# Hybrid decoder step on one core: the program is recorded first and issued in an order made by a list scheduler

## The chip, the core and the metric

The kernel runs on one core of a Trainium2 chip. The core has five instruction queues that run beside one another: PE (TensorE, matmuls; its weight loads are listed as PEld), DVE (VectorE), ACT (ScalarE), POOL (GpSimd) and SP (SyncE, which here issues the transfers between memory and SBUF). Each queue runs its instructions in the order in which they stand in it, and an instruction that waits for another engine holds up all that stand behind it. The metric is the device time of one execution in microseconds (us); lower is better.

## The reference

One decoder layer (D = 1024) over a prompt of 2048 tokens and, with the same weights, over one new token each of 8 sequences. Everything is float32.

```python
def decoder_layer(x, ...):
    y = parallel_mixer(rms_norm(x, norm_mix), ...)
    x = x + y
    x = x + memory_attend(rms_norm(x, norm_mem_q), mem_k, mem_v, w_mq, w_mo)
    x = x + swiglu(rms_norm(x, norm_ffn), w_gate, w_up, w_down)

def parallel_mixer(h, ...):
    p = h @ w_in
    u = p[GLU_A] * sigmoid(p[GLU_B])                 # Conformer half, 512 channels
    c = silu(layer_norm(depthwise_conv31(u) + conv_b))
    qkv = silu(depthwise_conv4(p[QKV]))              # gated DeltaNet half, 4 heads of 128
    q, k, v = l2_norm(q), l2_norm(k), v              # chunks of 64 tokens, triangular solve,
    o = gated_delta_chunked(q, k, v, g, beta, s0)    # 128x128 state handed from chunk to chunk
    return concat(c, rms_norm(o) * silu(z)) @ w_out

def memory_attend(h, mem_k, mem_v, ...):             # 4 heads of 256, 256 memory tokens
    return softmax(q @ mem_k.T * scale) @ mem_v @ w_mo

def swiglu(h, ...):                                  # inner width 2816
    return (silu(h @ w_gate) * (h @ w_up)) @ w_down
```

After the layer comes a last `rms_norm`; the outputs are the two sequences, the projected memory, and the new convolution rows and DeltaNet states.

## The kernel before

**Work.** The prompt is cut into 4 blocks of 512 tokens (`TB`). Per block the stages are: input projection (`hd`), short convolutions, the DeltaNet chunks, the 31-tap convolution, output projection and attention (`rg`, `sc`), and the feed-forward part (FFN). To keep float32's precision on TensorE's faster path, each operand is split into a rounded half and a remainder ("hi" and "lo"), and a product is made of three matmuls of halves. A weight tile arrives by transfer as `raw`; ACT writes its hi half and POOL or DVE its lo half into `w`. There are 11 `raw` and 6 `w` slots.

**FFN.** For each pair of 128-column steps the partial products `fx`, `fy` and `fz` are made on PE in PSUM banks of those names. DVE and ACT read them out into `ffu` and `ffs`, and PE needs the bank of a product free before it starts a later one: so PE's first matmul into `fy` can wait for a DVE operation on `ffs` or `ffu`. From the results `ff` the down products (`dn`) are made and added to the residual `x` by DVE (`xd` for the 8 decode rows).

**What runs beside it.** The next blocks' mixer: the convolution `cacc`, 31 taps of one `scalar_tensor_tensor` each on DVE (480 in all); the inverse of the DeltaNet triangle, long chains of short DVE operations on `bit`, `biq`, `w16` and `x16`; transposes of keys and queries on PE into `pk` and `pq`, four slices of 128 columns in one PSUM bank, of which ACT reads each slice for itself and sums its squares (`chj`); `lnq` and `podt` are other transposes of the same kind. `hT`, `catS` and `op` are operands as they are split on DVE, `sqj` squares for a norm, `kv`, `dg`, `chv`, `osc` smaller steps of the attention and of DeltaNet.

**Order.** The program is written by generators ("lanes") that the class `Sched` resumes. The classes `Clock` and `Engine` keep a virtual time for each engine with a cost for each operation, and a lane is resumed when the virtual PE has come so far that its inputs would be there. So the text of the program is already a merge of the FFN with the mixer of later blocks. Each call goes straight to the framework as it is written (`nc.tensor.matmul(...)`, line 256; `transpose`, line 261; DVE, ACT and POOL through `Engine`, line 118; transfers, line 243); the framework gives the tiles their slots, adds the semaphores, and orders each engine's queue by the place in the program. Since all calls pass through these few lines, the profile is read by tile names rather than by lines.

Of the kernel before, what the change touches and what calls it, by code (L numbers as in the profile page):

```python
# [8 lines left out]
F32 = mybir.dt.float32  # L9
F32R = mybir.dt.float32r  # L10
AF = mybir.ActivationFunctionType
ALU = mybir.AluOpType
# [35 lines left out]
NW = 6  # L48
NT2 = 28
NACT = 22  # L50
# [15 lines left out]
NRAW = 11  # L66


class Clock:


    def __init__(self):
        self.at = {"pe": 0.0, "act": 0.0, "dve": 0.0, "pool": 0.0, "sp": 0.0, "dma": 0.0}
        self.ready, self.used = {}, {}
        self.table = None
        self.ring, self.nbank = {}, {"mm": 3, "s": 3, "o": 1, "cv": 1}
        self.held = set()
# [20 lines left out]
SETS = {AF.Sigmoid: "sigmoid", AF.Silu: "silu", AF.Exp: "exp"}  # L98


def elems(ap):
    n = 1
    for x in ap.shape[1:]:
        n *= x
    return n


class Engine:
# [5 lines left out]
    def __getattr__(self, op):  # L114
        f = getattr(self.real, op)

        def call(**kw):
            r = f(**kw)  # L118
            ins = [v for k, v in kw.items() if k not in ("out", "accum_out") and hasattr(v, "name") and hasattr(v, "shape")]
            out = kw["out"]  # L120
            src = kw.get("in_", kw.get("in0"))
            n = max(elems(out), elems(src)) if src is not None else elems(out)
            if self.name == "act":
                ns = 80 + 0.86 * n + 93 * (len(ins) - 1) + (60 if kw.get("accum_out") is not None else 0)
                t = SETS.get(kw.get("func"))
                if t and t != self.clock.table:
                    self.clock.table = t
                    ns += 1290
            elif self.name == "dve":
                fast = op in ("tensor_copy", "tensor_scalar") and src.space != bass.MemoryType.PSUM  # L130
                ptr = any(hasattr(kw.get(k), "shape") for k in ("scalar", "scalar1"))
                ns = (125 if ptr else 65) + n * (6.2 if op == "reciprocal" else 0.53 if fast else 1.05)
            else:
                ns = 300 + n * 165 if kw.get("op") == ALU.pow else 120 + n * (2.2 if op == "tensor_tensor" else 3.4)
            self.clock.run(self.name, ns, ins, out)
            if kw.get("accum_out") is not None:
                self.clock.ready[kw["accum_out"].name] = self.clock.ready[out.name]
            return r

        return call  # L140


class Sched:


# [13 lines left out]
    def add(self, gen, slack=-20.0, first=False):  # L159

        lane = [gen, self.vt, gen.__name__, slack]
        self.lanes.insert(0 if first else len(self.lanes), lane)
        return lane
# [71 lines left out]
def hybrid_step(ctx: ExitStack, tc: tile.TileContext, i: dict, o: list):  # L235
    nc = tc.nc
    C = Clock()
    V, A, G = Engine(nc.vector, "dve", C), Engine(nc.scalar, "act", C), Engine(nc.gpsimd, "pool", C)
    GS = nc.gpsimd
    S = Sched(C)  # L240

    def dma(out, in_, after=0.0):
        nc.sync.dma_start(out=out, in_=in_)
        n = 4
        for x in out.shape:
            n *= x
        C.at["sp"] = max(C.at["sp"] + 60, C.when([in_]), after)
        C.at["dma"] = max(C.at["dma"], C.at["sp"] + 1100) + max(n / 360.0, 60.0)
        C.ready[out.name] = max(C.ready.get(out.name, 0.0), C.at["dma"] + 1650)
        C.used[in_.name] = max(C.used.get(in_.name, 0.0), C.at["dma"])  # L250

    def mm(out, lhsT, rhs, start, stop, skip=False):
        n = elems(rhs)
        four = lhsT.dtype == F32 or n < 256
        S.wait(max(C.when([lhsT, rhs]), C.ready.get("free " + out.name, 0.0) if start else 0.0))
        nc.tensor.matmul(out, lhsT, rhs, start=start, stop=stop, skip_group_check=skip)  # L256
        C.run("pe", 3 + max(n, 64) * (4 if four else 1) / 2.4, [lhsT, rhs], out, 90.0)

    def transpose(out, in_, identity):
        S.wait(max(C.when([in_]), C.ready.get("free " + out.name, 0.0)))  # L260
        nc.tensor.transpose(out, in_, identity)
        C.run("pe", 110.0, [in_], out, 90.0)

    cst = ctx.enter_context(tc.tile_pool(name="cst", bufs=1))
    sm = ctx.enter_context(tc.tile_pool(name="sm", bufs=2))
    wpool = ctx.enter_context(tc.tile_pool(name="wpool", bufs=NW))
    rpool = ctx.enter_context(tc.tile_pool(name="rpool", bufs=NRAW))
    t2pool = ctx.enter_context(tc.tile_pool(name="t2pool", bufs=NT2))
    cpool = ctx.enter_context(tc.tile_pool(name="cpool", bufs=2))
    apool = ctx.enter_context(tc.tile_pool(name="apool", bufs=NACT))  # L270
    psum = ctx.enter_context(tc.tile_pool(name="psum", bufs=1, space=bass.MemoryType.PSUM))
    dram = ctx.enter_context(tc.tile_pool(name="dram", bufs=1, space=bass.MemoryType.DRAM))
    W2 = 520

    uid = [0]
# [5 lines left out]
    live = {"t2": set(), "act": set()}  # L281
# [47 lines left out]
    def const(name, shape, dt=F32):  # L329
        return cst.tile(list(shape), dt, tag=name, name=name)  # L330
# [9 lines left out]
    def load_first(ks):  # L340
        for k in ks:
            dma(x_first[k], xT[k, :, cols_of(0)])
# [5 lines left out]
    vcol_t = const("vcol", [P, rows])  # L348
    load_first((0,))
    dma(vcol_t, i["vec"])  # L350
    ones = const("ones", [P, P])
    GS.memset(ones, 1.0)
    ident = const("ident", [P, P])
    make_identity(nc, ident)
    ex = const("ex", [P, 13])
    GS.memset(ex[:, 0:4], 0.5)
    GS.memset(ex[:, 4:8], -1.0)
    GS.memset(ex[:, 8:13], -0.5)
    nhalf = ex[:, 8:12]
# [44 lines left out]
    for pair in PAIRS:  # L404
        for st in STEPS:
            k = int(st[1])
            if st[0] == "h":
                at = [O_QKV // P + g + k for g in (H, 0, 2 * H)]
# [274 lines left out]
    def three(pts, wh, wl, x, spans, first, last, skip=False):  # L683
        for w_, part in ((wh, 0), (wh, 1), (wl, 0)):
            for pt, (lo, hi) in zip(pts, spans):
                mm(pt, w_, x[:, part, lo:hi], first and w_ is wh and part == 0, last and w_ is wl, skip)
# [7 lines left out]
    def rstd(sqs, n):  # L694

        yield sqs
        yield ("ps", "s")
        nt = n // P
        pt = ps("pss", shape=(P, nt))
        for t in range(nt):  # L700
            for k, s_ in enumerate(sqs):
                mm(pt[:, t : t + 1], s_[:, t * P : (t + 1) * P], ones[:, 0:1], k == 0, k == len(sqs) - 1)
        drop(*{s_.name: s_ for s_ in sqs}.values())
        m = small("ms", [P, nt], bufs=3)
        V.tensor_scalar(out=m, in0=pt, scalar1=1e-6, scalar2=None, op0=ALU.add)
        r = small("rs1", [P, nt], bufs=3)
        G.tensor_tensor(out=r, in0=m, in1=ex[:, 8 : 8 + nt], op=ALU.pow)
        yield r
        return r

    def spread(r, n, both=False, spare=RES):

        nt = n // P
        yield ("t2", 2 + spare)
        dg = t2("dg", (P, nt, P))
        rb_ = t2("rsb")[:, :n]
        V.tensor_tensor(out=dg, in0=bc(ident, 1, [P, nt, P]), in1=bc(r, 2, [P, nt, P]), op=ALU.mult)
        yield dg
        yield ("ps", "s")
        pb = ps("prs", shape=(P, n))  # L720
        mm(pb, ones, dg.rearrange("p t j -> p (t j)"), True, True)
        drop(dg)
        A.activation(out=rb_, in_=pb, func=AF.Copy)
        if both:
            return pb, rb_
        yield rb_
        return rb_
# [175 lines left out]
    def dec_mixer():  # L903
# [110 lines left out]
        for h in range(H):  # L1014
            transpose(pvt[:, h * P : (h + 1) * P], vhl[:, h, :].bitcast(F32), ident)
# [45 lines left out]
    def scalars(b, hT, res):  # L1061
# [12 lines left out]
        for t in range(NT):  # L1074
            transpose(pb_[:, t, :], bdf[:, t * P : (t + 1) * P], ident[:16, :16])
# [31 lines left out]
        yield ("ps", "s")  # L1107
        pr = ps("pgr", shape=(NT * H, P))
        transpose(pr, gcol.rearrange("p t h -> p (t h)"), ident)
        gr = t2("gr", (NT * H, P))  # L1110
        V.tensor_copy(out=gr, in_=pr)
# [114 lines left out]
    def base_inverse(x, w, tmp_):  # L1226

        GS.memset(w, 0.0)
        GS.memset(w[:, 0:256:17], 1.0)
        V.tensor_scalar(out=w[:, 1:256:34], in0=x[:, 1:256:34], scalar1=-1.0, scalar2=None, op0=ALU.mult)  # L1230
# [315 lines left out]
    for s in LEV:  # L1546
        m = const(f"nms{s}", [P, 64])
# [124 lines left out]
    for pair in PAIRS:  # L1672
# [3 lines left out]
        for st in STEPS:  # L1676
# [8 lines left out]
            k = int(st[1])  # L1685
# [692 lines left out]
    for b in range(NB):  # L2378
# [7 lines left out]
        rest = ffn(b, ops[b], go[b])  # L2386
        ws.pool_lo, ws.ahead = False, 4
    S.until(lambda: not S.lanes, "end")


_OUTS = [
# [76 lines left out]
```

## Time and profile before

| what | value |
| --- | --- |
| median of the runs (3) | 3152.3 us (3145.48 to 3153.3) |
| the profiled execution: its time | 3143.72 us |
| its span, first to last instruction | 3142.0 us |
| PE busy | 2981.1 us, 95% (18950 records; the program has 17905 matmuls, some leave two) |
| DVE busy | 2138.6 us, 68% |
| POOL busy | 1679.4 us, 53% |
| ACT busy | 1452.5 us, 46% |
| mean DMA rate | 149 GB/s |
| mean granted TensorE clock | 0.980 |

The span leaves 1.7 us of the execution's time outside of it. PE is the engine that is nearly always busy; the other engines deliver its operands and empty its banks. A row of the groups gives a kind of instruction, its total and mean duration, and the idle time just before it with the engine that ended it.

### The profile page before, as it was taken

The numbers are of one execution on the slowest core, as the hardware profiler recorded it, in microseconds if no ns is written. First come the engines' busy times: TensorE is split into PE (matmuls) and PEld (weight loads), VectorE is DVE, ScalarE is ACT, GpSimd is POOL, SyncE is SP. The second block draws the span as 40 slices with busy tenths as digits, with TensorE's granted clock in tenths as the row PEclk, the third lists the DMA queues.
The fourth block names the chain that finished last, engine by engine and source line by source line (L and its number), as shares of the span: only waits on it lengthen the run. The fifth ranks groups of instructions, "written<-read, shape, count | busy, mean of one in ns | idle before, by whom it ended". The sixth has DMA issues, their size and how long they took to land.

```text
span 3142.0 us, 53798 instructions
## 1 busy us (share of the span) xinstructions
PE 2981.1 (95%) x18950; PEld 2639.6 (84%) x18950; DVE 2138.6 (68%) x4335; ACT 1452.5 (46%) x2909; POOL 1679.4 (53%) x1454
## 2 busy tenths in 40 slices
PE   8999989999999989889989999999999999799998
PEld 6899967888887878778877888897799998689997
DVE  7767898978797889867778655446654445663435
ACT  6533444344663435344444545444444445444443
POOL 3423444334654557666731367883147775158786
PEclk9999999999999999999999999999999999999999
DMA  5433433443884335445557455553345443245452
GB/s 182 127 107 106 136 111 126 138 132 118 265 251 140 115 111 188 135 154 174 186 168 240 141 165 182 171 170 117 127 140 155 145 156 121 71 140 156 149 158 95
DMA packets 355182, 468.73 MB, mean 149 GB/s; under 512 B 56448, under 2 KB 154688, under 8 KB 354896
## 3 DMA queue, kind: packets, MB, share of 16 engines
q1 hardware_dynamic: 354912, 465.29, 46.7%
q8 instruction: 150, 2.46, 0.3%
q14 instruction: 120, 0.98, 0.1%
HBM read 380.18 MB, written 85.57 MB: 148 GB/s over the span
## 4 chain that ended last, share of the span: by engine, by line
PE 46%; DVE 9%; POOL 5%; issue 4%; DMA 2%; ACT 1%; SPq 0%; POOLq 0%; DVEq 0%; ACTq 0%
PE dn L256 12%; PE fy L256 10%; PE rg L256 7%; PE fz L256 6%; PE fx L256 6%; PE sc L256 3%; POOL w L118 3%; DVE w L118 1%; DVE x L118 1%; DVE op L118 1%; POOL sqj L118 1%; DVE tt L118 1%; DVE cacc L118 1%; DVE xn L118 1%; PE pu L256 1%
## 5 line engine op out<-in xcount | busy, mean ns | idle before, releaser
L118 POOL TENSOR_TENSOR w<-raw,w 128x512 fp32r<-128x512 f32 x898 | 1217.8, 1367 | 704.3 <-ACT w L118 649.7
L118 ACT ACTIVATE w<-raw 128x512 fp32r<-128x512 f32 x1176 | 735.0, 630 | 1024.4 <-PE dn L256 263.3
L256 PE MATMUL dn<-ff,w 128*128 128x512 f32 (+2 forms) x2688 | 524.1, 351 | 37.4 <-DVE xd L118 16.4
L256 PEld LDWEIGHTS dn<-ff,w 128*128 128x128 f32 x2688 | 426.8, 190 | 107.8 <-issue 23.1
L256 PE MATMUL fy<-op,w 128*128 128x256 f32 (+1 forms) x3168 | 434.9, 286 | 25.6 <-DVE ffs L118 12.2
L256 PEld LDWEIGHTS fy<-op,w 128*128 128x128 f32 x3168 | 406.2, 192 | 34.3 <-DVE ffu L118 14.3
L256 PE MATMUL hd<-hT,w 128*128 128x512 f32 (+2 forms) x1920 | 406.4, 360 | 15.3 <-ACT w L118 8.3
L118 DVE SCALAR_TENSOR_TENSOR cacc<-cu,cw,cacc 128x512 f32<-128x512 f32 x480 | 358.2, 746 | 9.2 <-ACT cacc L118 4.2
L256 PEld LDWEIGHTS hd<-hT,w 128*128 128x128 f32 x1920 | 305.1, 190 | 61.1 <-ACT w L118 8.4
L118 DVE TENSOR_TENSOR x<-dn,x 128x512 f32<-128x512 f32 (+1 forms) x448 | 252.5, 570 | 124.8 <-PE dn L256 123.4
L118 POOL TENSOR_TENSOR sqj<-sqj,sqj 128x512 f32<-128x512 f32 (+1 forms) x98 | 137.9, 1407 | 327.1 <-ACT sqj L118 322.1
L118 DVE TENSOR_TENSOR w<-raw,w 128x512 fp32r<-128x512 f32 x278 | 241.0, 874 | 101.5 <-ACT w L118 99.1
L256 PE MATMUL fz<-op,w 128*128 128x256 f32 (+1 forms) x2112 | 289.5, 285 | 3.3 <-DVE ffs L118 2.0
L256 PE MATMUL fx<-op,w 128*128 128x256 f32 (+1 forms) x2112 | 285.0, 283 | 4.4 <-ACT ffu L118 1.6
L256 PEld LDWEIGHTS fx<-op,w 128*128 128x128 f32 x2112 | 268.3, 189 | 13.0 <-ACT ffu L118 2.2
L256 PEld LDWEIGHTS fz<-op,w 128*128 128x128 f32 x2112 | 268.7, 190 | 6.3 <-DVE ffs L118 2.2
L256 PE MATMUL rg<-catS,w 128*128 128x512 f32 (+1 forms) x960 | 193.5, 357 | 4.3 <-DVE x L118 3.0
L256 PE MATMUL sc<-w,hT 128*128 128x512 f32 x768 | 190.8, 403 | 6.2 <-DVE x L118 4.4
L256 PE MATMUL rg<-pT,w 128*128 128x512 f32 x768 | 190.7, 403 | 3.5 <-ACT pr L118 3.1
L118 DVE TENSOR_TENSOR ffu<-fy,ffu 128x256 f32<-128x256 f32 (+1 forms) x176 | 74.3, 422 | 169.4 <-PE fy L256 169.0
L256 PEld LDWEIGHTS rg<-catS,w 128*128 128x128 f32 x960 | 155.4, 191 | 29.8 <-DVE x L118 2.7
L256 PEld LDWEIGHTS sc<-w,hT 128*128 128x128 f32 x768 | 143.0, 190 | 41.7 <-DVE x L118 5.0
(380 smaller groups left out, 4123.4 us busy)
## 6 DMA issues: line engine op xcount, KB each, us to landing
raw<-sums SPq DMA_DIRECT2D x264, 256.0 KB, 2.7
raw<-in_w_gate_dram SPq DMA_DIRECT2D x176, 256.0 KB, 2.7
raw<-in_w_down_dram SPq DMA_DIRECT2D x176, 256.0 KB, 2.6
raw<-in_w_up_dram SPq DMA_DIRECT2D x110, 256.0 KB, 2.6
raw<-in_w_in_dram SPq DMA_DIRECT2D x96, 256.0 KB, 2.8
sums<-raw SPq DMA_DIRECT2D x88, 256.0 KB, 2.0
raw<-in_w_out_dram SPq DMA_DIRECT2D x64, 256.0 KB, 3.8
raw<-wk SPq DMA_DIRECT2D x64, 256.0 KB, 2.7
```

The source lines that it names most:

```text
L118: r = f(**kw)
L256: nc.tensor.matmul(out, lhsT, rhs, start=start, stop=stop, skip_group_check=skip)
```

## The change

What each instruction computes is left alone. The calls that the program makes are no longer passed on, but recorded on a `Tape` with their engine, operands and a cost in ns. When the whole program has been written down, `Tape.graph` works out which operation depends on which, `Tape.order` makes a new order, and `Tape.issue` makes the calls in that order, with the framework's own ordering switched off (`manual_schedule`), so that every queue keeps the order of the calls. The framework still adds the semaphores.

- The graph: an operation depends on another where they touch overlapping boxes of rows and columns of the same tile, one of them writing; matmuls into the same PSUM tile keep their order.
- The order: an event-driven list scheduler. The engine that can start earliest takes, of the operations that are ready by its clock, the one that stands first in the program as it was written (`key`). A DVE operation that needs the port shared with POOL may be passed over for another that doesn't, while POOL holds the port. A tile may be begun only if its tag has a free slot, and no tile that stands before it in the program can be locked out.
- The clocks: costs per operation, a delay from each engine to each other one (`LAT`), 1283 ns for an ACT table load, transfers in a row at 360 bytes per ns.

```diff
+class Tape:
+    LAT = {
+        "pe": dict(pe=0, dve=196, act=197, pool=210, sp=180),
+        "dve": dict(pe=149, dve=127, act=128, pool=155, sp=120),
...
+    def cost(self, eng, op, args, kw, outs, ins):
...
+            return max(max(m, 64) * 0.835, (n if n >= 256 else 4 * n) * 0.4492) + 3, False, None
...
+        if eng == "act":
+            ptr = len(ins) - 1
+            return 0.834 * n + (50 if psum_in else 94) + 93 * ptr, False, SETS.get(kw.get("func"))
...
+            return 68 + (61 if ptr else 0) + n * (6.2 if op == "reciprocal" else 0.525 if half else 1.042), big > 1, None
...
+        return 135 + n * (2.14 if op == "tensor_tensor" else 3.4), True, None
...
+    def graph(self):
+        over = lambda x, y: x[0] <= y[1] and y[0] <= x[1] and x[2] <= y[3] and y[2] <= x[3]
...
+            for a in outs:
+                if a.name in self.tag_of:
+                    b = self.box(a)
+                    for k, x in writes.get(a.name, ()):
+                        if over(b, x):
+                            p[k] = 1
+                    for k, x in reads.get(a.name, ()):
+                        if over(b, x):
+                            p[k] = 1
+                    if eng == "pe":
+                        if a.name in last_pe:
+                            p[last_pe[a.name]] = 1
+                        last_pe[a.name] = n
...
+    def order(self, key=None):
+        preds, tiles = self.graph()
+        key = key or list(range(N))
...
+        while len(done) < N:
+            best = None
+            for e in engines:
+                if avail[e]:
+                    t = clock[e]
+                elif future[e]:
+                    t = max(clock[e], future[e][0][0])
+                else:
+                    continue
+                if best is None or t < best[0]:
+                    best = t, e
...
+            ns, port, tb = self.ops[n][7]
+            s = t
+            if port and e in ("dve", "pool"):
+                s = max(s, port_at)
+                port_at = s + ns
...
+    def issue(self, tc):
+        with tc.manual_schedule():
+            for n in self.order():
+                _, _, fn, args, kw, *_ = self.ops[n]
+                fn(*args, **kw)
...
 def hybrid_step(ctx: ExitStack, tc: tile.TileContext, i: dict, o: list):
...
-    V, A, G = Engine(nc.vector, "dve", C), Engine(nc.scalar, "act", C), Engine(nc.gpsimd, "pool", C)
+    tape = Tape()
+    GS, PE, SP = tape.port(nc.gpsimd, "pool"), tape.port(nc.tensor, "pe"), tape.port(nc.sync, "sp")
...
-        nc.tensor.matmul(out, lhsT, rhs, start=start, stop=stop, skip_group_check=skip)
+        PE.matmul(out, lhsT, rhs, start=start, stop=stop, skip_group_check=skip)
...
     S.until(lambda: not S.lanes, "end")
+    tape.issue(tc)
```

The instructions are the same ones as before, but for their waits and the ACT table loads, which follow from the order (67 before, 72 now). Of PE's 17907 instructions 14348 (80%) stand at the same place of their queue as before; of DVE's, which move most after ACT's, 758 do, and the mean move is 10 places.

**Place 1: DVE, in an FFN that runs beside a triangle's inverse and a convolution; PE's `fy` waits here at 1269 us of the profile before.** `bit`, `biq`, `w16` and `x16` belong to the inverse, `cacc` to the convolution, `w` from `raw` is a weight's lo half; `ffs` from `fy` is what PE waits for. Before:

```order
L118 TENSOR_TENSOR ffu_2601_13745<-fz_2603_13748,ffu_2601_13745 128x256
L118 TENSOR_TENSOR bit_2574_13605<-w16_2569_13565,x16_2568_13564 32x512
L118 SCALAR_TENSOR_TENSOR cacc_2618_13834<-cu_2586_13640,cw_124,cacc_2618_13834 128x512
L118 TENSOR_REDUCE biq_2597_13720<-bit_2574_13605 32x64
L118 SCALAR_TENSOR_TENSOR cacc_2618_13834<-cu_2586_13640,cw_124,cacc_2618_13834 128x512
L118 TENSOR_TENSOR bit_2574_13605<-biq_2597_13720,w16_2569_13565 32x512
L118 TENSOR_TENSOR w_2617_13831<-raw_2609_13798,w_2617_13831 128x512
L118 TENSOR_REDUCE w16_2569_13565<-bit_2574_13605 32x8x8
L118 TENSOR_TENSOR w_2619_13841<-raw_2583_13632,w_2619_13841 128x512
L118 COPY x16_2568_13564<-w16_2569_13565 32x256
L118 SCALAR_TENSOR_TENSOR cacc_2618_13834<-cu_2586_13640,cw_124,cacc_2618_13834 128x512 x4
L118 TENSOR_TENSOR ffs_2602_13746<-ffu_2601_13745,fy_2608_13775 128x256
```

Now:

```order
L426 TENSOR_TENSOR ffu_2601_2799<-fz_2603_2801,ffu_2601_2799 128x256
L426 TENSOR_TENSOR bit_2574_2772<-biq_2592_2790,w16_2569_2767 32x4x4
L426 SCALAR_TENSOR_TENSOR cacc_2618_2816<-cu_2586_2784,cw_107,cacc_2618_2816 128x512
L426 TENSOR_TENSOR bit_2574_2772<-biq_2592_2790,w16_2569_2767 32x4x4
L426 TENSOR_TENSOR ffs_2602_2800<-ffu_2601_2799,fy_2608_2806 128x256
L426 TENSOR_REDUCE w16_2569_2767<-bit_2574_2772 32x2x2 x4
L426 SCALAR_TENSOR_TENSOR cacc_2618_2816<-cu_2586_2784,cw_107,cacc_2618_2816 128x512
L426 TENSOR_TENSOR bit_2574_2772<-w16_2569_2767,x16_2568_2766 32x64
L426 SCALAR_TENSOR_TENSOR cacc_2618_2816<-cu_2586_2784,cw_107,cacc_2618_2816 128x512
L426 TENSOR_TENSOR bit_2574_2772<-w16_2569_2767,x16_2568_2766 32x64
L426 TENSOR_REDUCE biq_2595_2793<-bit_2574_2772 32x16 x2
L426 TENSOR_TENSOR ffs_2602_2800<-fz_2603_2801,ffs_2602_2800 128x256
```

The operation on `ffs` and `fy` stood behind the last steps of the inverse, two weight halves and six taps that followed the operation on `ffu`, and stands behind two short operations and one tap now; nineteen operations went from ahead of it to behind it, those before the first row shown among them, and one tap went the other way.

**Place 2: DVE, in a later FFN; PE's `dn` waits here at 2136 us.** `hT` and `catS` are operands of a later stage, `x` from `dn` is the addition to the residual, and `ffu` from `fy` is what frees the bank. Before:

```order
L118 TENSOR_TENSOR ffu_4310_23069<-fz_4314_23090,ffu_4310_23069 128x256
L118 TENSOR_TENSOR ff_4315_23098<-ffu_4290_22933,ff_4315_23098 128x512
L118 TENSOR_TENSOR hT_4334_23230<-x_3426_18165,hT_4334_23230 128x512
L118 TENSOR_TENSOR ffs_4311_23070<-ffu_4310_23069,fy_4318_23112 128x256
L118 TENSOR_TENSOR ffs_4311_23070<-fz_4314_23090,ffs_4311_23070 128x256
L118 TENSOR_TENSOR ffu_4310_23069<-fy_4318_23112,ffu_4310_23069 128x256
L118 TENSOR_TENSOR x_2204_11735<-dn_4327_23187,x_2204_11735 128x512
L118 TENSOR_TENSOR x_2210_11758<-dn_4328_23195,x_2210_11758 128x512
L118 TENSOR_TENSOR sqj_4335_23233<-sqj_4335_23233,sqj_4355_23310 128x512
L118 TENSOR_TENSOR ffu_4310_23069<-fy_4318_23112,ffu_4310_23069 128x256
```

Now:

```order
L426 TENSOR_TENSOR ffu_4310_4508<-fz_4314_4512,ffu_4310_4508 128x256
L426 TENSOR_TENSOR ff_4315_4513<-ffu_4290_4488,ff_4315_4513 128x512
L426 TENSOR_TENSOR hT_4354_4552<-x_3433_3631,hT_4354_4552 128x512
L426 TENSOR_TENSOR ffs_4311_4509<-ffu_4310_4508,fy_4318_4516 128x256
L426 TENSOR_TENSOR catS_4465_4663<-cat_4464_4662,catS_4465_4663 128x512
L426 TENSOR_TENSOR ffs_4311_4509<-fz_4314_4512,ffs_4311_4509 128x256
L426 TENSOR_TENSOR catS_4467_4665<-cat_4466_4664,catS_4467_4665 128x512
L426 TENSOR_TENSOR ffu_4310_4508<-fy_4318_4516,ffu_4310_4508 128x256
L426 TENSOR_TENSOR x_2204_2402<-dn_4327_4525,x_2204_2402 128x512
L426 TENSOR_TENSOR catS_4469_4667<-cat_4468_4666,catS_4469_4667 128x512
L426 TENSOR_TENSOR x_2210_2408<-dn_4328_4526,x_2210_2408 128x512
L426 TENSOR_TENSOR ffu_4310_4508<-fy_4318_4516,ffu_4310_4508 128x256
```

Three operations on `catS` of 512 columns now stand ahead of the second `ffu` from `fy`, and one on `sqj` went behind it.

**Place 3: PE, in an input projection (at 127.78 us of the profile before), with the waits.** Four transposes of keys (`kT`) go into slices of one bank, `pk`. Before:

```order
L256 MATMUL hd_250_1540<-hT_69_441,w_194_1192 128x264
L256 MATMUL hd_249_1539<-hT_69_441,w_194_1192 128x256
L256 MATMUL hd_250_1540<-hT_69_441,w_194_1192 128x264
L261 MATMUL pk_254_1602<-ident_94,kT_235_1470 128x128 [waits DMAHW5_49]
L261 MATMUL pk_254_1602<-ident_94,kT_235_1470 128x128 x3
L256 MATMUL hd_249_1539<-hT_71_447,w_194_1192 128x256
L256 MATMUL hd_250_1540<-hT_71_447,w_194_1192 128x264
```

Now:

```order
L426 MATMUL hd_249_446<-hT_69_266,w_194_391 128x256
L426 MATMUL hd_250_447<-hT_69_266,w_194_391 128x264
L426 MATMUL pk_254_451<-ident_91,kT_235_432 128x128 [waits DMAHW1_49]
L426 MATMUL pk_254_451<-ident_91,kT_235_432 128x128 x2
L426 MATMUL pk_254_451<-ident_91,kT_235_432 128x128 [waits Activation_49]
L426 MATMUL hd_249_446<-hT_71_268,w_194_391 128x256
L426 MATMUL hd_250_447<-hT_71_268,w_194_391 128x264
```

The last of the four now waits for ACT, which it did not: an ACT operation that reads another slice of the bank (`chj`) has been issued ahead of it. A transpose into `pk`, `pq`, `lnq`, `pkk` or `podt` has such a new wait at 21 places (8, 6, 4, 1 and 2), at none before.

More of the change, by code (lines that the diff above doesn't have):

```diff
@@ new lines, with __init__, __getattr__, call @@
+class TapePort:
+    def __init__(self, tape, real, eng):
+        self.tape, self.real, self.eng = tape, real, eng
+    def __getattr__(self, op):
+        fn = getattr(self.real, op)
+        def call(*args, **kw):
+            self.tape.add(self.eng, op, fn, args, kw)
+        return call
+class TapePool:
+    def __init__(self, tape, pool, bufs, psum):
+        self.tape, self.real, self.bufs, self.psum = tape, pool, bufs, psum
+    def tile(self, shape, dt, tag, name, bufs=None):
+        t = self.real.tile(shape, dt, tag=tag, name=name) if bufs is None else self.real.tile(shape, dt, tag=tag, name=name, bufs=bufs)
+        tp = self.tape
+        key = (id(self), tag)
+        tp.tag_of[t.name] = key
+        tp.bufs[key] = bufs or self.bufs
+        if self.psum:
+            tp.psum.add(t.name)
+        return t
@@ L237, in hybrid_step @@
     C = Clock()
-    V, A, G = Engine(nc.vector, "dve", C), Engine(nc.scalar, "act", C), Engine(nc.gpsimd, "pool", C)
-    GS = nc.gpsimd
+    tape = Tape()
+    GS, PE, SP = tape.port(nc.gpsimd, "pool"), tape.port(nc.tensor, "pe"), tape.port(nc.sync, "sp")
+    V, A, G = Engine(tape.port(nc.vector, "dve"), "dve", C), Engine(tape.port(nc.scalar, "act"), "act", C), Engine(GS, "pool", C)
     S = Sched(C)
     def dma(out, in_, after=0.0):
-        nc.sync.dma_start(out=out, in_=in_)
+        SP.dma_start(out=out, in_=in_)
         n = 4
@@ L260, in transpose @@
         S.wait(max(C.when([in_]), C.ready.get("free " + out.name, 0.0)))
-        nc.tensor.transpose(out, in_, identity)
+        PE.transpose(out, in_, identity)
         C.run("pe", 110.0, [in_], out, 90.0)
[L264 to L272, printed above, removed]
+    cst = tape.pool(ctx.enter_context(tc.tile_pool(name="cst", bufs=1)), 1)
+    sm = tape.pool(ctx.enter_context(tc.tile_pool(name="sm", bufs=2)), 2)
+    wpool = tape.pool(ctx.enter_context(tc.tile_pool(name="wpool", bufs=NW)), NW)
+    rpool = tape.pool(ctx.enter_context(tc.tile_pool(name="rpool", bufs=NRAW)), NRAW)
+    t2pool = tape.pool(ctx.enter_context(tc.tile_pool(name="t2pool", bufs=NT2)), NT2)
+    cpool = tape.pool(ctx.enter_context(tc.tile_pool(name="cpool", bufs=2)), 2)
+    apool = tape.pool(ctx.enter_context(tc.tile_pool(name="apool", bufs=NACT)), NACT)
+    psum = tape.pool(ctx.enter_context(tc.tile_pool(name="psum", bufs=1, space=bass.MemoryType.PSUM)), 1, True)
+    dram = tape.pool(ctx.enter_context(tc.tile_pool(name="dram", bufs=1, space=bass.MemoryType.DRAM)), 1)
     W2 = 520
```

210 lines of the change are left out of this document (added).

## The prediction

> **What bounds the kernel now.** I read the engine shares first, then the slices, the groups, the waits of PE and the timeline at the largest of them. The shares:
>
> ```profile
> PE 2981.1 (95%) x18950; PEld 2639.6 (84%) x18950; DVE 2138.6 (68%) x4335; ACT 1452.5 (46%) x2909; POOL 1679.4 (53%) x1454
> ```
>
> PE sets the time, and a new order cannot take work from it, since the matmuls stay the same. It can only fill PE's idle time, 3142.0 - 2981.1 = 161 us, and what the clock loses behind it. Where that lies, six windows tell (length, PE busy, its loads, DVE, ACT, POOL, then granted clock, DMA share, GB/s):
>
> ```profile
> 0.00:1000.00 1000.00, 954.97 (x5835) 824.07 (x5836) 821.87 (x1821) 472.64 (x1005) 422.19 (x498) 0.99 0.48 150
> 1000.00:1700.00 700.00, 639.14 (x3878) 555.61 (x3877) 555.97 (x968) 310.78 (x655) 391.05 (x308) 0.96 0.49 160
> 1700.00:2700.00 1000.00, 977.15 (x6394) 878.68 (x6393) 536.97 (x1096) 476.48 (x897) 580.43 (x431) 0.99 0.47 149
> 2300.00:2600.00 300.00, 300.00 (x2478) 298.66 (x2477) 132.11 (x398) 139.39 (x254) 228.81 (x171) 1.00 0.50 153
> 2700.00:2800.00 100.00, 79.02 (x531) 72.67 (x530) 74.77 (x187) 38.07 (x64) 30.18 (x23) 0.88 0.27 85
> 2800.00:3100.00 300.00, 300.00 (x2123) 281.05 (x2121) 124.71 (x215) 140.88 (x258) 235.01 (x176) 1.00 0.52 157
> ```
>
> Two FFN stretches of 300 us are PE from end to end at full clock: nothing is to be had there. Up to 1700 us, where DVE is 81% busy (1377.84 of 1700), PE idles 105.9 us; from 1700 to 2700 another 22.9, and 21.0 in the single piece from 2700 to 2800. PE's waits say for whom (total, times, longest):
>
> ```profile
> PE dn L256 <- DVE xd L118: 16.4, 2, 13.6
> PE fy L256 <- DVE ffs L118: 12.2, 2, 6.5
> PE fy L256 <- DVE ffu L118: 12.0, 13, 3.8
> PE dn L256 <- DVE ffu L118: 9.7, 3, 4.2
> PE pss L256 <- DVE sqj L118: 8.4, 6, 3.2
> PE hd L256 <- ACT w L118: 8.3, 2, 7.3
> ```
>
> Nearly all are DVE's, and short: no engine is too slow, but DVE does other work when PE needs a bank. So the change is worth what it does to the place of these few DVE operations in their queue.
>
> **Gains.** The 6.5 us row is place 1 of the change. The timeline there, DVE's rows and then PE's:
>
> ```profile
> 1262.57 1.00 DVE L118 TENSOR_TENSOR bit<-biq,w 32x512 f32<-32x512 f32 x1
> ...
> 1265.58 3.11 DVE L118 SCALAR_TENSOR_TENSOR cacc<-cu,cw,cacc 128x512 f32<-128x512 f32 x4
> 1268.60 0.41 DVE L118 TENSOR_TENSOR ffs<-ffu,fy 128x256 f32<-128x256 f32 x1
> ```
>
> ```profile
> 1259.31 1.68 PE L256 MATMUL fz<-op,w 128*128 128x256 f32 x12 [0.17 <-DVE ffu L118]
> ...
> 1269.06 2.93 PE L256 MATMUL fy<-op,w 128*128 128x256 f32 x12 [6.53 <-DVE ffs L118]
> ```
>
> DVE ran inverse steps and taps while PE stood; the operation PE waited for takes 0.41. The nineteen operations that go behind it last 8.77 us here, one tap of 0.75 comes ahead: 8.0 against a stall of 6.5, so it closes. What is late next: the inverse steps, whose result PE needs only in a later chunk, and the taps, which have slack until the convolution ends.
>
> I did the same for each of the 104 gaps of PE over 0.3 us that end on DVE, ACT or POOL, together 162.0 us, the first of them inside the first of these rows, the last in the second:
>
> ```profile
> 7.34 2.09 PE L256 MATMUL hd<-hT,w 128*128 128x512 f32 x4 [7.34 <-ACT w L118]
> ...
> 3133.88 1.19 PE L256 MATMUL prs<-dg,ones 128*128 128x256 f32 x2 [1.58 <-DVE dg L118]
> ```
>
> For each I took the operation waited for, with what stood ahead of it in its queue before and doesn't now, and the reverse, and likewise PE's own work moved ahead of the waiting matmul, in durations of this trace. At 55 gaps (80.3 us of stall) the balance is better, and it covers 72.1 us, 43 of them whole. At 8 (20.0 us) nothing moves. One of these is the longest of all, 13.6 us before `dn` at 2749.76:
>
> ```profile
> 2746.72 0.68 DVE L118 TENSOR_TENSOR op<-xn,op 128x512 fp32r<-128x512 f32 x1
> 2747.32 1.28 DVE L118 TENSOR_TENSOR op<-tt,op 128x512 fp32r<-128x512 f32 x2
> 2748.53 0.68 DVE L118 TENSOR_TENSOR w<-raw,w 128x512 fp32r<-128x512 f32 x1
> 2749.13 0.41 DVE L118 TENSOR_TENSOR x<-dn,x 128x256 f32<-128x256 f32 x1
> 2749.47 0.14 DVE L118 TENSOR_TENSOR xd<-dn,xd 128x4 f32<-128x4 f32 x1
> ```
>
> A norm's whole work stands ahead of `x` and `xd` there, in both kernels, so that stall stays. **Term 1: -72.** That is the most these places give; below it lies nothing at all, if what DVE has passed over becomes the next wait.
>
> **Losses.** At the other 41 gaps (61.7 us) more now stands ahead than before, by 132.6 us in all. Place 2 is one:
>
> ```profile
> 2129.61 2.48 PE L256 MATMUL dn<-ff,w 128*128 128x512 f32 x10
> 2136.31 4.09 PE L256 MATMUL dn<-ff,w 128*128 128x512 f32 x10 [4.21 <-DVE ffu L118]
> ```
>
> ```profile
> 2126.53 0.69 DVE L118 TENSOR_TENSOR x<-dn,x 128x512 f32<-128x512 f32 x1 [0.71 <-PE dn L256]
> 2134.18 1.73 DVE L118 TENSOR_TENSOR sqj<-sqj,sqj 128x512 f32<-128x512 f32 x1 [6.96 <-POOL sqj L118]
> 2135.84 0.41 DVE L118 TENSOR_TENSOR ffu<-fy,ffu 128x256 f32<-128x256 f32 x1
> ```
>
> `hT` and `catS` operations of 4.1 us come ahead there and `sqj` (1.73) goes behind. But DVE stood idle for 6.96 us just before, waiting for POOL with `sqj` at the head of its queue; if the work moved ahead runs in that time it costs nothing, and `ffu` even goes earlier. Bounds for the 132.6: nearly none (a twentieth, 7), or all. I take a fifth, 27, because the list fills time in which its clock sees DVE free, and its costs agree with rows of this trace where I can hold them together:
>
> ```profile
> L256 PE MATMUL dn<-ff,w 128*128 128x512 f32 (+2 forms) x2688 | 524.1, 351 | 37.4 <-DVE xd L118 16.4
> L118 DVE SCALAR_TENSOR_TENSOR cacc<-cu,cw,cacc 128x512 f32<-128x512 f32 x480 | 358.2, 746 | 9.2 <-ACT cacc L118 4.2
> L118 POOL TENSOR_TENSOR w<-raw,w 128x512 fp32r<-128x512 f32 x898 | 1217.8, 1367 | 704.3 <-ACT w L118 649.7
> ```
>
> It charges 233 ns for a 512-column matmul, and the ten at 2129.61 took 2.48 with the last one's drain in it; 662 for a tap, of 746 measured with its overlap; 1231 for POOL's half, of 1367. Errors of a tenth stay within a gap's length where the order was made with DVE free, but DVE is 81% busy before 1700 us, so not all of it can be. **Term 2: +27.**
>
> **New waits.** At 21 places PE now waits between two transposes for a reader of another slice of the same bank (place 3). Before, these readers came when they could. What one such wait costs, the keys' transposes show, first all of them, then place 3's own in the timeline and by tile:
>
> ```profile
> L261 PE MATMUL pk<-ident,kT x64: 270/272/329, 99.9 to 1347.4; 128*128 128x128 f32 x64
> L118 ACT ACTIVATE chj<-pk x64: 252/277/278, 103.2 to 1353.2; 128x128 bf16<-128x128 f32 x64
> L118 ACT ACTIVATION_READ_ACCUMULATOR chj<-pk x64: 191/195/214, 103.3 to 1353.4; 128x1 f32 x64
> ```
>
> ```profile
> 127.78 0.60 PE L261 MATMUL pk<-ident,kT 128*128 128x128 f32 x4
> ```
>
> ```profile
> L118 ACT ACTIVATE chj<-pk x4: 258/272/277, 134.9 to 138.3; 128x128 bf16<-128x128 f32 x4
> ```
>
> If ACT is there at once, PE loses the read's 0.28 us: 21 x 0.28 = 6. If ACT is as late as it was before, it loses that lateness: 3.3 us at the first group of four, 5.8 at the last, 7.1 at place 3, and 3.4 on average over the 32 groups of keys and queries: 21 x 3.4 = 71. Everything in PE's queue stands behind such a wait, the projection's matmuls above all. In the new order ACT's `chj` stands directly behind one weight half (0.63, first row below), no longer behind an activation that itself waited for DVE, so I take a read with its accumulator (0.28 + 0.20) and that half ahead of it, 1.1 to 1.2 us each: **term 3: +25**, nearer to the low end for that reason.
>
> ```profile
> L118 ACT ACTIVATE w<-raw 128x512 fp32r<-128x512 f32 x1176 | 735.0, 630 | 1024.4 <-PE dn L256 263.3 <-issue 151.1 <-PE rg L256 110.1
> L118 ACT ACT_TABLE_LOAD x67 | 86.0, 1283 | 10.6 <-DMA vcol<-in_vec_dram 4.8 <-issue 2.8 <-DVE du L118 1.8
> ```
>
> The Trainium skill speaks against the change here: its page "PSUM — Partial Sum Buffer", section "PSUM bank collisions raise a hardware error", asks that PSUM be guarded by bank and quadrant, not by address, whichever engines read or write. The change's graph goes by address, so by that rule its list counts on overlaps that it will not get. The 21 waits in the new order agree; with a price of 3.4 us each for them the sum is that of the third rival below.
>
> **Clock.** Behind 1269.06 the twelve matmuls took 2.93 us, the twelve at 1259.31 took 1.68: a stop that long costs some 1.25 us more in clock. Seven gaps of over 3 us are closed whole: 7 x 1.25 = 9. **Term 4: -9**, between 0 (new stops as long) and -25 (the 0.96 of 1000 to 1700 loses 28 us, most of it regained).
>
> The Trainium skill's page "TensorE: Matmul & The Clock Gate", Part 1, has the clock halved only after an idle window of about 3.4 us. By that rule just three of the seven stops would have cost anything; term 4 would be an estimated -4, and the sum 3119.7. The 6.53 us stop agrees with it, and none of the rows here tells the two counts apart.
>
> **The rest.** Five more table loads cost ACT 5 x 1.28 by the second row above, on an engine 46% busy. SP issues as many transfers as before, and DMA at half its share covers their new places; its queue is in order, so a load that waits for a `raw` slot holds those behind it, and if that made a weight late, ACT's `w` and PE's `hd` would be late with it, as the 7.3 us in the row of `hd` and ACT's `w` shows. Recording the program happens before the chip runs and costs it nothing.
>
> **Sum**, against the profiled execution: 3143.7 - 72 + 27 + 25 - 9 = 3114.7. The median of the runs stands 8.6 above that execution, so 3123 for the median.
>
> **Rivals.**
> *DVE has no room.* Of the work moved ahead four fifths count, as DVE is 81% busy up to 1700 us: -72 + 106 + 25 - 9 = +50, 3202. It decides from a share of 42% on ((72 + 9 - 25) / 132.6). For it: the busiest windows are those in which most of this work lies. Against it: DVE's idle time there, 322 us, is more than twice the 132.6.
> *The waits only move.* 80% of PE's instructions keep their place, ties go by the old program order, and a filled stall hands the wait to the next thing that is late; gains halve, -36 + 27 + 10 = about 0: 3143 to 3161 for the median. The 43 gaps closed whole speak against it.
> *ACT is late at the new waits.* Term 3 is 71: -72 + 27 + 71 - 9 = +17, 3169. For it: 7.1 us at place 3. Against it: what stands ahead of `chj` on ACT has changed.
>
> **How the numbers follow.** The forecast has 0.53, no room 0.14, only moving 0.19, late ACT 0.14. Low end: -72 + 7 + 6 - 25 = -84, 3068, and a little under it, 3062. High end: past late ACT, short of no room in full, 3190. The forecast's own range is 3068 to 3145. Under 0.3% (9.5 us) a measurement can't tell from no change: faster takes the forecast and a little of only moving, 0.57; same the most of only moving and a little of the others, 0.19; slower no room and most of late ACT, 0.24.
>
> **What would show it.** PE busy close to 2972 and its idle time down to some 140 us; the `fy <- ffs` row of the waits down from 12.2 to about 6; the `xd` row still at 16; new rows of PE `pk` and `pq` waiting for ACT `chj`, with 25 us or less; the granted clock of 1000 to 1700 up from 0.96; `dn <- ffu` not longer than 9.7. The prediction is wrong if the rows of `pk` and `pq` exceed 50, or if PE's waits for DVE up to 1700 us sum to no less than before.

## The result, and the profile after

| | before | changed |
| --- | --- | --- |
| median of the runs | 3148.89 us (3143.52 to 3153.3, 4 runs) | 3058.68 us (3057.51 to 3060.09, 4 runs) |
| span of the profiled execution | 3142.0 us | 3058.4 us |
| mean granted clock | 0.980 | 0.989 |

The ratio is 0.9714, with a 95% interval of 0.9696 to 0.9733: 90 us faster, where 29 were forecast, and 3 us below the range's low end. One of the four executions of `e6b_dve_dear` below took 10861 us at a granted clock of 0.376, and its ratio leaves that one out. The shares of the changed kernel:

```profile
PE 2956.4 (97%) x18950; PEld 2622.1 (86%) x18950; DVE 2146.3 (70%) x4335; ACT 1468.3 (48%) x2914; POOL 1699.7 (56%) x1454
```

PE's idle time fell from 160.9 to 102.0 us and its busy time by 24.7: the span's 83.6. The same stretches as before (length, PE, its loads, DVE, ACT, POOL, clock, DMA share, GB/s), though the work in them stands up to 84 us earlier at the end:

```profile
0.00:1000.00 1000.00, 954.98 (x5819) 818.52 (x5819) 812.27 (x1812) 483.41 (x1003) 420.64 (x497) 0.99 0.48 150
1000.00:1700.00 700.00, 680.97 (x4137) 593.25 (x4138) 590.24 (x1050) 333.66 (x702) 412.06 (x317) 0.99 0.53 172
1700.00:2700.00 1000.00, 974.78 (x6553) 888.53 (x6552) 574.77 (x1188) 488.62 (x908) 595.76 (x434) 0.99 0.46 146
```

Most of the gain lies between 1000 and 1700 us, where PE was idle for 60.9 us and is for 19.0, and the clock is 0.99 instead of 0.96. PE's idle time in the first 1000 us stayed the same. PE's waits (total, times, longest), the first five, then what stood high before or is new:

```profile
PE dn L426 <- DVE xd L426: 15.7, 2, 13.2
PE hd L426 <- ACT w L426: 7.7, 2, 5.7
PE sc L426 <- ACT pr L426: 6.0, 2, 3.5
PE pq L426 <- ACT chj L426: 5.3, 7, 1.3
PE pk L426 <- ACT chj L426: 4.0, 8, 0.5
...
PE pss L426 <- DVE sqj L426: 3.7, 1, 3.7
...
PE lnq L426 <- ACT lny L426: 2.5, 4, 0.8
...
PE fy L426 <- DVE ffu L426: 1.5, 2, 0.9
```

`fy` for `ffs` (12.2 before, about 6 forecast) and `dn` for `ffu` (9.7 before) have gone from the list, `fy` for `ffu` fell from 12.0 to 1.5, and `xd` stays. Place 1 now, PE and then DVE:

```profile
1251.22 1.58 PE L426 MATMUL fz<-op,w 128*128 128x256 f32 x12
1252.64 1.57 PE L426 MATMUL fy<-op,w 128*128 128x256 f32 x12
```

```profile
1250.61 0.40 DVE L426 TENSOR_TENSOR ffs<-ffu,fy 128x256 f32<-128x256 f32 x1
1250.94 0.34 DVE L426 TENSOR_REDUCE w<-bit 32x4 f32<-32x8 f32 x4
1251.22 0.73 DVE L426 SCALAR_TENSOR_TENSOR cacc<-cu,cw,cacc 128x512 f32<-128x512 f32 x1
```

`ffs` is done 1.6 us before PE comes to `fy`, and the last steps of the inverse and the taps follow it. Place 2, which the prediction counted as a loss:

```profile
2067.17 6.13 PE L426 MATMUL dn<-ff,w 128*128 128x512 f32 x26
```

```profile
2061.77 1.44 DVE L426 TENSOR_TENSOR catS<-cat,catS 128x512 fp32r<-128x512 f32 x1
...
2063.47 1.45 DVE L426 TENSOR_TENSOR catS<-cat,catS 128x512 fp32r<-128x512 f32 x1
...
2065.77 0.86 DVE L426 TENSOR_TENSOR catS<-cat,catS 128x512 fp32r<-128x512 f32 x1
2066.55 0.68 DVE L426 TENSOR_TENSOR x<-dn,x 128x512 f32<-128x512 f32 x1
2067.37 0.42 DVE L426 TENSOR_TENSOR ffu<-fy,ffu 128x256 f32<-128x256 f32 x1
2067.71 0.84 DVE L426 TENSOR_TENSOR sqj<-sqj,sqj 128x512 f32<-128x512 f32 x1
```

26 matmuls run without a stop where PE stood for 4.21 us. Before, `sqj` stood ahead of `ffu` and held DVE's queue for 6.96 us while it waited for POOL. Now `sqj` stands behind `ffu`, and `ffu` is done 3.5 us before the matmul that needs it. The three `catS` operations run further ahead, where DVE before had four gaps of 0.48 to 0.99 us in front of this wait.

A second place shows the same. `fy` waited 5.68 us at 1368.28 before, and DVE's queue in front of the operation waited for (`ffs` from `fy`) was held up by POOL:

```profile
1362.88 0.69 DVE L118 TENSOR_TENSOR dn<-pvv,s 128x512 f32<-128x512 f32 x1 [4.73 <-POOL s L118]
...
1367.21 0.69 DVE L118 TENSOR_TENSOR osc<-po,fc 128x512 f32<-128x512 f32 x1 [0.61 <-POOL fc L118]
1367.82 0.41 DVE L118 TENSOR_TENSOR ffs<-ffu,fy 128x256 f32<-128x256 f32 x1
```

In the changed kernel the wait for `s` is 1.58 us, `osc` stands behind `ffs`, and PE goes from `fz` to `fy` without a stop, though 2.05 us of other work came ahead of `ffs` and only the 0.69 of `osc` went behind. The forecast had left this stall standing (`fy` for `ffs` at about 6).

Matching every matmul of one trace with the same one of the other gives this account, whose first three rows are the prediction's 104 places. A gap is what lies between the starts of two matmuls above the usual time of the first one's shape, and over 0.3 us (the last row has what is smaller):

| us of PE's gaps | before | changed | difference | forecast |
| --- | --- | --- | --- | --- |
| 55 places with a better balance | 80.3 | 8.9 | -71.4 | -72 |
| 41 places with work moved ahead | 61.7 | 14.5 | -47.2 | +27 |
| 8 places with none moved | 20.0 | 17.2 | -2.8 | 0 |
| all other gaps | 21.1 | 76.4 | +55.3 | +25 |
| below 0.3 us, slow clock among it | 57.6 | 41.0 | -16.6 | -9 |

### The profile page after: what moved, and what is told of

Its sections match the earlier page's. It is cut to its first block, busy times and chain, and to the rows that moved or that the text cites. A ratio compares the mean times of both kernels' runs of the same rounds, so it can differ in the third digit from the quotient of the medians.

```text
span 3058.4 us, 53895 instructions
## 1 busy us (share of the span) xinstructions
PE 2956.4 (97%) x18950; PEld 2622.1 (86%) x18950; DVE 2146.3 (70%) x4335; ACT 1468.3 (48%) x2914; POOL 1699.7 (56%) x1454
## 5 line engine op out<-in xcount | busy, mean ns | idle before, releaser
L426 POOL TENSOR_TENSOR w<-raw,w 128x512 fp32r<-128x512 f32 x898 | 1232.2, 1382 | 616.0 <-ACT w L426 522.3
L426 PEld LDWEIGHTS dn<-ff,w 128*128 128x128 f32 x2688 | 427.0, 190 | 84.0 <-issue 16.6
L426 PE MATMUL fy<-op,w 128*128 128x256 f32 (+1 forms) x3168 | 428.0, 283 | 2.0 <-DVE ffu L426 1.5
L426 PE MATMUL rg<-catS,w 128*128 128x512 f32 (+2 forms) x960 | 190.8, 354 | 4.1 <-DVE w L426 2.2
```

What stands on the lines that cost most here:

```text
L426: fn(*args, **kw)
```

## The experiments

Every ratio below is to the kernel before, run on the same chip beside it; that of the changed kernel is 0.9714.

| run | median us | ratio, 95% interval |
| --- | --- | --- |
| s1_before_order | 3151.6 | 1.0007 (0.9997 to 1.0016) |
| s2_only_dve | 3172.0 | 1.0067 (1.0047 to 1.0086) |
| s7_only_pe | 3132.3 | 0.9945 (0.9930 to 0.9960) |
| s4_all_but_pe | 3104.3 | 0.9859 (0.9838 to 0.9880) |
| s13_pe_dve | 3096.5 | 0.9826 (0.9809 to 0.9842) |
| s11_all_but_sp | 3095.8 | 0.9829 (0.9815 to 0.9844) |
| e6_dve_cheap | 3231.4 | 1.0256 (1.0241 to 1.0271) |
| e6c_dve_tenth | 3103.2 | 0.9854 (0.9835 to 0.9873) |
| e6b_dve_dear | 3131.1 | 0.9938 (0.9921 to 0.9954) |
| g1_no_port | 3136.8 | 0.9954 (0.9939 to 0.9968) |
| g2_no_lat | 3177.0 | 1.0076 (1.0059 to 1.0093) |
| e5_bank | 3040.8 | 0.9655 (0.9640 to 0.9669) |
| h1_fine | 3046.4 | 0.9652 (0.9636 to 0.9668) |
| f1_bank_evac30 | 3055.7 | 0.9697 (0.9676 to 0.9718) |
| f1_bank_evac100 | 3058.6 | 0.9711 (0.9697 to 0.9726) |
| f1_bank_evac300 | 3076.0 | 0.9763 (0.9747 to 0.9779) |
| f2_bank_feed100 | 3274.1 | 1.0394 (1.0379 to 1.0410) |

### Is it the order at all? (s1)

`WAS`, in this and the next group, is a table of the order in which the operations of the kernel before started.

```diff
-            for n in self.order():
+            for n in was():
```

> The recording as in the changed kernel, issued with the framework's ordering off, but in the order in which the kernel before was seen to start its operations (9 DVE pairs swapped where the address boxes ask for it). Theory 'order' (the whole gain is the new order of the queues): within 0.3% of the kernel before, 3139 to 3158 us. Rival 'issue' (the gain comes from switching off the framework's ordering, or from other slots and semaphores): below 3100 us.

It is the kernel before to 0.1%. So recording and switching off the framework's ordering neither cost nor bring anything that can be measured; the 90 us are order.

### Which queue's order? (s2, s7, s4, s13, s11)

The list is made as in the change, but the queues named keep the order of the kernel before: an operation on such an engine comes up only when the one ahead of it has been placed. The graph is built from that order too, while the rank stays the written one. A list of this kind that holds no queue was not run, so the losses against the changed kernel have that difference in them.

```diff
+        w = was()
+        self.ops = [self.ops[n] for n in w]
         preds, tiles = self.graph()
...
-        key = key or list(range(N))
+        key = key or list(w)
...
+        for n in range(N):
+            e = self.ops[n][0]
+            if e in ("pe", "act", "pool", "sp"):      # s2; s7: all but pe; s4: pe; s13: act, pool, sp; s11: sp
+                if e in prev:
+                    chain[prev[e]] = n
+                    left[n] += 1
+                prev[e] = n
```

> PE, ACT, POOL and SP keep the queue order of the kernel before; only DVE's queue is made by the list. Theory 'DVE' (the banks that PE waits for come free earlier): at least two thirds of the gain of 90 us, 3090 us or less. Rival 'PE' (PE's own matmuls moved into its gaps): less than a third, 3120 us or more.

> PE keeps the queue order of the kernel before, the other four queues are made by the list. Theory 'DVE': nearly all of the gain, 3075 us or less. Rival 'PE': less than half of it, 3105 us or more.

> Only PE's queue is made by the list, the other four keep the order of the kernel before. Theory 'DVE': 3125 us or more. Rival 'PE': 3100 us or less.

> PE's and DVE's queues are made by the list; ACT, POOL and SP keep the order of the kernel before. Theory 'pair' (PE and DVE wait mostly for each other, so the two together hold the gain): 3085 us or less. Rival 'joint' (every queue must be ordered by the same clock; ACT, POOL and the transfers left in the old order make new waits): 3105 us or more.

> All queues made by the list but SP's, whose transfers keep the order of the kernel before. Theory 'joint': the transposing transfers of the DeltaNet inverse (zt to Tm) come late against the moved DVE work, 3080 us or more. Rival 'pair': as the changed kernel, 3055 to 3068 us.

Theory "DVE" fell: DVE's new order alone is slower than before, by 21 us. Its rival fell as well: PE's new order alone gives 17 us of the 90, and everything but PE 45. PE's and DVE's together gave 3096.5, between the forecasts of "pair" and "joint". With SP's old transfer order 37 us of the gain are lost, as "joint" had it, but not for its reason: PE waits 1.4 us for the transposing transfers there (`pu` for `Tm`; 1.6 in the changed kernel), and what rose are waits for ACT, `pq`, `pk` and `lnq` to 6.7, 6.2 and 5.8 and `dr` for `w` to 7.8. How the transfers' order makes these was not followed up. PE's waits with DVE's order alone:

```profile
PE pss L451 <- DVE sqj L451: 21.7, 7, 6.2
PE pu L451 <- DMA Tm<-zt: 18.5, 4, 9.2
PE dn L451 <- DVE xd L451: 16.7, 2, 14.1
```

The `fy` rows are small here too (3.0 for `ffs`, 3.1 for `ffu`), but PE waits for the transposing transfer of the inverse (`Tm` from `zt`), which SP issues at its old place, and for `sqj`. In the accounting above the 55 places fall to 34.7 us and the 41 to 40.2, and the other gaps rise from 21.1 to 113.7; with all five queues they rise to 76.4. Closing the old waits is not enough: the new ones have to be kept away, and none of the parts tried gains as much as all five queues together.

### What makes the work moved ahead free? (e6, e6c, e6b, g1, g2)

The list's clock is made wrong, the rest is the change.

```diff
-            return 68 + (61 if ptr else 0) + n * (...), big > 1, None
+            return 0.7 * (68 + (61 if ptr else 0) + n * (...)), big > 1, None    # e6; e6c: 0.9, e6b: 1.3
```

```diff
-            if port and e in ("dve", "pool"):
+            if False:                           # g1, and no passing over of an operation
```

For g1 the condition for passing an operation over is switched off in the same way. For g2 the numbers of `LAT` are 0, but for those of transfers.

> The list takes every DVE operation as 0.7 of its cost. Theory 'clock' (work moved ahead costs nothing because the list's clock is right about when DVE is free): 20 us or more above the changed kernel, 3079 us or more. Rival 'any order' (ties by the written order and waiting for inputs do it, the costs matter little): 3050 to 3070 us.

> The list takes every DVE operation as 1.3 of its cost. Theory 'clock' (any error of the list's clock puts work where PE needs the engine): 20 us or more above the changed kernel, 3079 us or more. Rival 'one side' (only a cost taken too low hurts; a cost taken too high leaves DVE air): 3050 to 3072 us.

> The list takes every DVE operation as 0.9 of its cost. The prediction held that errors of a tenth stay within a gap's length. Theory 'tolerant': 3055 to 3070 us, as the changed kernel. Rival 'drift' (the error adds up along a busy DVE, and 0.7 cost 173 us): a third of that or more, 3110 us or more.

> The list takes DVE and POOL as free of each other: no shared port, and no passing over. Theory 'clock': DVE's long operations beside POOL's come out later than the list thinks, 3075 us or more. Rival 'tolerant': within 12 us of the changed kernel, up to 3070 us.

> The list takes every delay between engines as 0 (transfers keep theirs). Theory 'clock': the chains of short operations come out later than the list thinks, 3075 us or more. Rival 'tolerant': up to 3070 us.

"Clock" held in the four runs that it was put to. In e6c "tolerant" fell, and 3103.2 stayed short of the 3110 of "drift". Costs a tenth too low on DVE take 44 us of the 90, costs of 0.7 turn the gain into a loss of 2.6%, and too high a cost hurts as well. Without the port 76 us go by the ratios, and without the list's delays of 0.06 to 0.21 us between engines all of the gain. PE's waits with DVE at 0.7:

```profile
PE pk L426 <- ACT chj L426: 22.6, 10, 6.8
PE dn L426 <- DVE xd L426: 16.2, 2, 13.7
PE pq L426 <- ACT chj L426: 13.7, 10, 4.7
PE prs L426 <- DVE dg L426: 10.4, 7, 4.1
```

Three of these four rows were small or absent with the right costs, and PE's gaps outside the 104 places sum to 192.2 us, against 76.4. The rows for `chj` are what the rival "ACT is late" described, 36 us here, and those for DVE what "no room" did: at costs this wrong both come about.

### The waits within a bank (e5, h1)

```diff
     def box(self, a):
+        if a.name in self.psum:
+            return 0, P - 1, 0, 511
```

> The list's graph takes a PSUM tile as one box, so that a transpose and the reader of another slice depend on each other and the list sees the wait. Theory 'bank' (the new waits of pk, pq and lnq for ACT, 11.8 us in the profile of the changed kernel, are lost time): 5 to 12 us under the changed kernel, 3047 to 3054 us. Rival 'hidden' (PE would have waited a little later anyway, or the bank-wise order gives up as much overlap): 3055 to 3065 us.

"Bank" held in its direction, and its size was too small: e5 gains 18 us, and the intervals of the two ratios lie apart (0.9640 to 0.9669, and 0.9696 to 0.9733). PE's waits for these tiles:

```profile
PE pq L428 <- ACT chj L428: 5.2, 3, 2.9
...
PE lnq L428 <- DVE lnx L428: 2.1, 2, 1.2
...
PE pkk L428 <- ACT chj L428: 1.4, 1, 1.4
```

`pk` no longer waits for `chj`, nor `lnq` for `lny`, while `pq` waits as long in fewer pieces. PE's gaps over 0.3 us fell by 11.8 and those below by 4.3. Of the 18 us, the waits by name account for at most 5; that the rest is a list that no longer runs ahead of the chip after each such wait fits the group above, but was not shown. It is the fastest of all kernels here together with the next one.

h1 adds to it costs that agree with the changed kernel's times from start to start: 16 ns more for ACT from SBUF, 20 or 100 more with a running sum, 223 for float32 matmuls of 128 columns instead of 236.

> The bank-wise graph with three costs set to the times from start to start in the profile of the changed kernel: ACT from SBUF 16 ns more, ACT with a running sum 20 or 100 ns more, float32 matmuls of 128 columns 223 instead of 236. Theory 'clock' (the rest of the gain lies in what is still wrong in the list's clock): under the bank-wise graph by 5 us or more, 3036 us or less. Rival 'floor of the method' (what is left is shared ports and places such as xd, which costs don't reach): 3036 to 3050 us.

The ratio is the same as e5's (0.9652 and 0.9655), as "floor of the method" had it. Finer costs of this kind bring nothing that can be measured; what makes the floor was not tested.

### Another rank for what PE waits for (f1, f2)

`xd` is left as the longest stall, 13 us behind a norm on DVE. Ranking DVE's reads of PSUM earlier should end it. All four runs have the graph by bank.

```diff
-        key = key or list(range(N))
+        key = key or [n - 100 * (o[0] == "dve" and any(a.name in self.psum for a in o[6]))   # 30, 300
+                      for n, o in enumerate(self.ops)]
```

For f2 every operation on which PE depends directly gets the 100 places.

> The bank-wise graph, and a DVE operation that reads PSUM ranks 100 places earlier in the list. Theory 'evacuation' (the 15.4 us of PE for xd, behind a norm's work on DVE, and the other waits for DVE reads of PSUM go): 10 to 25 us under the bank-wise graph, 3016 to 3031 us. Rival 'passed over' (what is passed over, the norm and the inverse, is late next, as in the run with DVE's queue alone): 3036 us or more.

> The same with 300 places. Theory 'evacuation': within 6 us of the run with 100. Rival 'passed over': 10 us or more above the run with 100.

> The bank-wise graph, and every operation on which a PE operation depends directly ranks 100 places earlier, on all engines. Theory 'evacuation' (PE's direct predecessors first is what counts): 3031 us or less. Rival 'passed over': 3036 us or more.

> The bank-wise graph, and a DVE operation that reads PSUM ranks 30 places earlier. With 100 places it was 3058.6, with none 3040.8. Theory 'passed over': 3038 us or more, no gain from it at any size. Rival 'evacuation, in a small dose': 3033 us or less.

"Passed over" won at each size: by the ratios 13, 18 and 34 us above e5 for 30, 100 and 300 places, and f2 is slower than the kernel before by 3.9%. The waits with 100 places:

```profile
PE dn L428 <- DVE xd L428: 10.3, 4, 4.5
PE hd L428 <- ACT w L428: 8.0, 2, 6.3
PE rg L428 <- DVE w L428: 6.7, 1, 6.7
PE pod L428 <- DVE kvT L428: 5.6, 1, 5.6
```

The longest wait for `xd` fell from 12.9 (e5) to 4.5 as meant, and all of them from 15.4 to 10.3. In its place `rg` for a weight on DVE rose from 2.1 to 6.7 and `pod` for `kvT` from 1.9 to 5.6. So leaving the written order as the rank cost more than it brought each time it was tried.

## Why the prediction was wrong

- **Direction and cause: right.** PE's short waits for DVE operations that stood behind other work; s1 shows that the order is all of it. DVE's order alone does not do it, though (s2): that the change is worth what it does to a few DVE operations in their queue was too narrow.
- **Term 1 (-72): right in size**, -71.4 at these 55 places. Place 1 closed, and the `xd` stall stayed at 13.2 us, both as said. The balance of moved work that chose the 55 is not confirmed by it: the 41 places that it called worse lost about three quarters of their stalls, against nine tenths here. That the size came out is in part luck.
- **Term 2 (+27): the step that failed.** It added up the durations of what was moved ahead of an operation in its queue, and took a fifth of them as lost. At these places the stalls fell by 47.2 us instead. The sum left out the time in which the queue itself stood still: 6.96 us at place 2, which the text names, and 4.73 us in front of `ffs` before 1368 us, both for POOL and both gone or shorter in the new order. Work moved ahead into DVE's idle time cost nothing there, an operation that waits stood in front no longer or waited less, and the queue behind it came earlier rather than later. That is shown at these two places. It is not all of it: at about half of the places where more work came ahead, the engine's idle time in the 10 us before was shorter than that work, and most of these stalls closed too. Why they did stays open. e6, e6c, e6b, g1 and g2 show that it depends on the list's costs, port and delays being right. The error of this term, 74 us, is larger than the whole miss of 61.
- **"Errors of a tenth stay within a gap's length": wrong**, also with the reserve that the prediction made for a busy DVE. e6c has an error of that size and loses half of the gain. The change's own costs did not have it for a tap: the 0.746 us of the trace overlaps the next operation, as the prediction says, and from start to start a tap with other work behind it takes 0.65 (with another tap behind it 0.79, last section), against 0.662 in the list. The difference was still counted as an error that the list tolerates.
- **Term 3 (+25): twice too high.** The waits of `pk`, `pq` and `lnq` for ACT measure 5.3 + 4.0 + 2.5 = 11.8 us, or 0.6 each over the 19 times in their rows, against 1.2. But the other gaps grew by 55.3 in all, of which the prediction had only this part: other new waits, at places that had none, were not in the sum, and took back most of what the 41 places gave.
- **Term 4 (-9): too small.** PE's busy time fell by 24.7, about the end of its range, and the small gaps by 16.6; from 1000 to 1700 us the clock went from 0.96 to 0.99. Eleven stops of over 3 us closed instead of seven, and three others came or grew past it. The price of a stop was also low: behind 1269.06 the granted clock stayed at 0.50 up to 1273.8, and 22 matmuls took 4.83 us where 22 at the changed kernel's 1.42 us for twelve take 2.60, so this stop cost 2.2 us and not 1.25. Whether only the longest stops count, which the prediction left open, the clock tells: it was 0.50 from 1683.5 to 1686.8 us, behind a stop of 3.10 us, and from 2635.8 to 2639.1, behind one of 3.24, but 1.00 from 1596.4 to 1602.0, behind one of 3.35. So shorter stops can cost clock, and the length of a stop alone does not decide it.
- **The rivals.** "No room" did not come (its 3202 is passed only with wrong costs or another rank, e6 and f2). "The waits only move" came in part: 55 of the 121 us closed at the 104 places came back elsewhere. "ACT is late" did not come with the change's own costs.
- **The Trainium skill's rule** in "PSUM — Partial Sum Buffer", section "PSUM bank collisions raise a hardware error", to guard PSUM by bank and not by address, bears on this change as the prediction said: PE waited for ACT at 19 of the transposes that share a bank with a reader, and the same list with a graph by bank is 18 us faster. What the rule guards against, an error raised by the hardware, no run here shows.

## What to carry to other kernels

When a list scheduler orders a kernel, its clock has to be right: without the delays between engines, or with one engine's costs at 0.7, the whole gain was lost, without the shared port most of it, and costs a tenth too low on one engine took half. Leaving the written order as the rank cost 13 us or more, and in f2 more than the whole gain. Order all queues by the one clock, since DVE's queue ordered alone closed its old waits and opened others, and give the graph the dependences that the chip's program will really have, banks included. In a forecast, do not price work that moves ahead by the length of the queue alone: look for idle time in front of it and for waits of the queue itself, and count the waits that will arise where there were none.

## What the runs showed of the hardware

A tap (`cacc`) with another tap directly behind it takes longer than one with other work behind it. In the kernel before, the four in a row from 1265.58 to the next operation's start at 1268.60 took 3.02 us. In the changed kernel a tap with other work behind it took 0.65 from its start to the next (DVE's timeline):

```profile
1243.98 0.73 DVE L426 SCALAR_TENSOR_TENSOR cacc<-cu,cw,cacc 128x512 f32<-128x512 f32 x1
1244.63 0.67 DVE L426 TENSOR_TENSOR x<-dn,x 128x512 f32<-128x512 f32 x1
```

With 0.65 for the last of the four, the first three took 0.79 each. Over the whole trace of the kernel before, the medians are 0.79 with a tap behind and 0.66 with other work behind. All taps in a row write and read the same tile; whether that is the reason was not tested. Such pairs fell from 141 to 110 with the new order, which is only 31 x 0.13 = 4 us of DVE's time.
